# Modulation steps at six places of each feed-forward group, bias rows written in four pieces, and five operations moved to VectorE

## The chip, the cores and the metric

The kernel runs on one core of a Trainium2 chip. The core has five engines with an instruction queue each: TensorE (PE, matrix products; its weight loads are listed as PEld), VectorE (DVE), ScalarE (ACT), GpSimd (POOL) and SyncE (SP, which here only issues DMAs). Each engine takes its own instructions strictly in order; engines wait for one another through semaphores. The metric is the device time of one execution in microseconds (us).

## The reference

A diffusion backbone of two layers over 256 latent and 256 context tokens, width 1024, all in float32.

```python
def _swiglu(h, wg, wu, wd):
    return (jax.nn.silu(h @ wg) * (h @ wu)) @ wd

def reference(x, c, ctx, c_ctx, ...):
    for i in range(DEPTH):
        sh1, sc1, gt1, sh2, sc2, gt2 = _adaln(c, w_mod[i], b_mod[i])   # silu(c) @ w_mod + b_mod, six pieces
        cmod = _adaln(c_ctx, w_mod[i], b_mod[i])
        h_lat = _modulate(_rmsnorm(x, g_norm1[i]), sh1, sc1)
        h_ctx = _modulate(_rmsnorm(ctx, g_norm1[i]), cmod[0], cmod[1])
        if i % 2 == 0:
            y_lat, y_ctx = _mixer_ab(h_lat, h_ctx, ...)      # GQA beside chunked gated linear attention
            ffn = dense SwiGLU, D_FF = 3584
        else:
            y_lat, y_ctx = _mixer_c(h_lat, h_ctx, ...)       # neighbourhood attention + relative bias rpb_c
            ffn = top-2-of-8 expert SwiGLU
        x = x + gt1 * y_lat
        x = x + gt2 * ffn(_modulate(_rmsnorm(x, g_norm2[i]), sh2, sc2))
        ...                                                  # the same for ctx, in layer 0
    return _rmsnorm(x, g_final)
```

## The kernel before

The stages follow one another: layer 0's mixer (to about 345 us of the span), the dense feed-forward network (345 to 842), the norm of layer 1 and the projection of its values `vc` (842 to 910), neighbourhood attention (910 to 1060), router and experts (1060 to 1990).

A float32 product is written as three matmuls of rounded operands (`mm3`, L213 to L216; `mm3_features`, L476 to L481): high times high, high times low, low times high. So each weight tile is loaded (`raw`, a 1 MB DMA on SP's queue, L168), rounded on ACT (`whi`, L201), and its remainder is taken by one DVE subtraction of 2048 columns (`wlo`, L203). For four numbered tiles (`ON_POOL`: 8, 12, 57 and 71) the subtraction runs on POOL instead, in eight pieces of 256 columns (L209). Tile 8 is the first half of the weights of the `rb` projection (its matmuls write `pt_rb`); tile 57 is the second of the two weight tiles of the first half of `vc` (`pt_vc`).

The feed-forward network runs in seven groups (`NG`) of 512 hidden columns, about 62 us each. The up part of a group multiplies by gate and up weights (`pf_fg`, `pf_fu`), then `sg` (silu on ACT L965, product on DVE L966) and its two parts `fT` (L967, L968); the down part runs over four token blocks `t` and two halves: twelve matmuls into a bank `fd`, then `rtmp_ff` (DVE, L734, frees the bank) and `xr` (DVE, L735). A call of `tick()` in the group steps a generator: it computes three pieces of layer 1's modulation vector, pieces (1,0), (1,1) and (1,2). A piece takes ten steps: start the first 1 MB load of `w_mod`; eight chunks, in each of which DVE multiplies the chunk by a column of the condition and adds it into `acc` (L286 for the first, L288 after it; for piece (1,0) four half-wide operations, since both conditions need it); and an end with eight small matmuls into `mod_ps` (L294), `m_sb` (L301), four transposes `modT_ps` (L304) and two copies to `mT` (L308). Before, `tick()` stands behind each second `j` of an even group and behind each `j` of an odd one, twenty in all; `tick(24)` behind the loop runs what is left.

Then `norm_stream` makes layer 1's input for both token streams (transposes `tf_n` on PE, `f_hi` on ACT, `tfraw_n` on either, `f_lo` on DVE L380), and `proj_tokens` computes `vc` in two halves, each of two weight tiles. The relative bias goes a way of its own on POOL's queue: a table `rb_s` is zeroed (L997), sixteen small loads fill it (L999), one DMA writes each row 64 times to device memory as `rb_d` (L1000, 7168 rows of 512 bytes), each pair of heads reads its `bias` from there by four DMAs (L1055), and a window mask is added in three pieces on POOL (L1058). The zeroing and the load of the router's weights `wrA` are held until the write of `rb_d` is issued.

A scheduler orders the instructions of each engine; the code marked `ahead(PREP)` is weight preparation that it may issue early, and `issue_after(x)` holds an instruction until `x` has been issued.

## Time and profile before

| | us |
|---|---|
| three runs | 2011.80, 2011.66, 2010.35 |
| median | 2011.66 |
| the profiled execution | 2009.91 |
| its span in the trace | 2007.9 |
| PE busy | 1934.4 (96%) |
| DVE busy | 744.7 (37%) |
| ACT busy | 448.1 (22%) |
| POOL busy | 170.6 (8%) |

Times of the trace are us from the start of the span. A timeline row gives the start, the duration, engine, line, operation, `written<-read`, and in brackets the idle time of the engine just before it with what ended it. A matmul's duration is its whole way through the array; the step from one start to the next is what it costs in a row of matmuls. PE's granted clock is 1.00 at 2.4 GHz.

### The profile page before, as it was taken

The page shows a single profiled execution, that of the slowest core. Times are in us where ns is not written, and L with a number is a line of the kernel's source. Part 1 is how long each engine was busy: PE and PEld are TensorE (multiplying, and loading weights), DVE is VectorE, ACT ScalarE, POOL GpSimd, SP SyncE. Part 2 cuts the span into 40 slices and gives each one's busy share as a digit, 9 for nine tenths or more (in the row PEclk, how much of TensorE's full clock was granted, in tenths as well). Part 3 has the DMA queues.
Part 4 walks back from the last instruction along what each step waited for, and adds up shares of the span by engine and source line. Part 5 has one row for each costly group of instructions (what it writes and reads, how often), then busy time and mean ns, then how long its engine had stood idle before and what let it go on. Part 6 is the DMA issues. An engine that isn't in the chain of part 4 may idle for free.

```text
span 2007.9 us, 37143 instructions
## 1 busy us (share of the span) xinstructions
PE 1934.4 (96%) x16627; PEld 1180.6 (59%) x16627; DVE 744.7 (37%) x1185; ACT 448.1 (22%) x732; POOL 170.6 (8%) x203
## 2 busy tenths in 40 slices
PE   6998998999999999789999999999999999999996
PEld 3665676888878888567765354545444444544433
DVE  3246587576445643836773101111020101111022
ACT  4232265422222222235553010000100001010001
POOL 1103010000000000433311000000000100001010
PEclk9999999999999999899999999999999999999998
DMA  8624120454243442653338999999999999999991
GB/s 331 223 95 168 52 76 24 166 168 142 89 140 118 135 154 84 210 140 100 108 113 312 399 406 375 379 404 390 383 381 399 398 384 362 380 408 389 402 395 46
DMA packets 118901, 493.32 MB, mean 246 GB/s; under 512 B 10656, under 2 KB 50912, under 8 KB 98256
## 3 DMA queue, kind: packets, MB, share of 16 engines
q1 hardware_dynamic: 114096, 481.04, 63.2%
q0 software_dynamic: 3216, 7.03, 1.4%
q8 instruction: 132, 2.16, 0.4%
q10 hardware_dynamic: 1424, 2.81, 0.4%
q14 instruction: 33, 0.27, 0.0%
HBM read 486.13 MB, written 4.72 MB: 244 GB/s over the span
## 4 chain that ended last, share of the span: by engine, by line
PE 91%; DVE 3%; ACT 2%; issue 2%; DMA 1%; POOL 1%; ACTq 0%; SPq 0%; POOLq 0%; DVEq 0%
PE pu_e L1306 15%; PE pg_e L1306 14%; PE py_e L1306 14%; PE pf_fu L479 3%; PE pf_fu L480 3%; PE pf_fu L481 3%; PE pf_fg L479 3%; PE pf_fg L480 3%; PE pf_fg L481 3%; PE fd L216 2%; PE fd L215 2%; PE fd L214 2%; PE sc_e L1381 1%; PE mod_ps L253 1%; PE o_c L859 1%
## 5 line engine op out<-in xcount | busy, mean ns | idle before, releaser
L1306 PE MATMUL pu_e<-raw,X_all 128*32 128x448 f32 x3072 | 306.1, 540 | 0.0
L1306 PE MATMUL py_e<-raw,eT_e 128*32 128x256 f32 x5376 | 296.5, 379 | 0.0
L1306 PE MATMUL pg_e<-raw,X_all 128*32 128x448 f32 x3024 | 291.4, 539 | 0.0
L1306 PEld LDWEIGHTS py_e<-raw,eT_e 128*32 128x32 f32 x5376 | 190.4, 110 | 105.1 <-issue 5.1
L1306 PEld LDWEIGHTS pg_e<-raw,X_all 128*32 128x32 f32 x3024 | 100.0, 110 | 181.2 <-issue 175.6
L1306 PEld LDWEIGHTS pu_e<-raw,X_all 128*32 128x32 f32 x3072 | 98.4, 110 | 182.4 <-issue 178.6
L203 DVE TENSOR_TENSOR wlo<-raw,whi 128x2048 fp32r<-128x2048 f32 (+1 forms) x67 | 153.0, 2293 | 123.4 <-ACT whi L201 123.3
L201 ACT CAST whi<-raw 128x2048 fp32r<-128x2048 f32 (+1 forms) x73 | 135.0, 1859 | 262.4 <-PE fd L216 116.8
L1343 DVE TENSOR_TENSOR m_sb<-m_sb,pu_e 128x448 f32<-128x448 f32 x48 | 27.9, 604 | 393.5 <-PE pu_e L1306 393.4
L1339 ACT ACTIVATE m_sb<-pg_e 128x448 f32<-128x448 f32 x48 | 26.1, 543 | 512.8 <-PE pg_e L1306 512.8
L1384 POOL TENSOR_TENSOR xr<-xr,ytmp_e 128x512 f32<-128x512 f32 x28 | 35.2, 1277 | 822.5 <-DVE ytmp_e L1383 822.5
L481 PE MATMUL pf_fg<-f_hi,wlo 128*128 128x512 f32 (+1 forms) x240 | 92.2, 384 | 1.9 <-DVE wlo L203 1.9
L479 PE MATMUL pf_fg<-f_hi,whi 128*128 128x512 f32 (+1 forms) x240 | 93.1, 388 | 0.6 <-ACT whi L201 0.6
L214 PE MATMUL fd<-whi,fT 128*128 128x512 f32 x224 | 89.2, 398 | 4.3 <-DVE rtmp_ff L734 4.3
L480 PE MATMUL pf_fg<-f_lo,whi 128*128 128x512 f32 (+1 forms) x240 | 92.2, 384 | 0.2 <-DVE f_lo L380 0.2
L481 PE MATMUL pf_fu<-f_hi,wlo 128*128 128x512 f32 (+1 forms) x240 | 91.9, 383 | 0.0
L479 PE MATMUL pf_fu<-f_hi,whi 128*128 128x512 f32 (+1 forms) x240 | 91.2, 380 | 0.5 <-ACT whi L201 0.5
L480 PE MATMUL pf_fu<-f_lo,whi 128*128 128x512 f32 (+1 forms) x240 | 91.5, 381 | 0.0
L216 PE MATMUL fd<-whi,fT 128*128 128x512 f32 x224 | 89.6, 401 | 0.0
L215 PE MATMUL fd<-wlo,fT 128*128 128x512 f32 x224 | 89.3, 399 | 0.0
L1383 DVE SCALAR_TENSOR_TENSOR ytmp_e<-sc_e,comb,gate 128x512 f32<-128x512 f32 x32 | 23.6, 749 | 165.3 <-PE sc_e L1381 160.5
L1374 ACT COPY yF<-py_e 32x256 f32<-32x256 f32 x48 | 17.4, 362 | 265.9 <-PE py_e L1306 231.3
(375 smaller groups left out, 2715.9 us busy)
## 6 DMA issues: line engine op xcount, KB each, us to landing
raw<-in_w_moe_up_dram SPq DMA_DIRECT2D x128, 896.0 KB, 6.6
raw<-in_w_moe_down_dram SPq DMA_DIRECT2D x112, 1024.0 KB, 8.6
raw<-in_w_moe_gate_dram SPq DMA_DIRECT2D x126, 896.0 KB, 7.6
raw<-in_w_mod_dram SPq DMA_DIRECT2D x48, 1024.0 KB, 5.0
raw<-in_w_ff_gate_dram SPq DMA_DIRECT2D x14, 1024.0 KB, 5.0
raw<-in_w_ff_up_dram SPq DMA_DIRECT2D x14, 1024.0 KB, 5.0
raw<-in_w_ff_down_dram SPq DMA_DIRECT2D x14, 1024.0 KB, 4.8
raw<-in_w_in_c_dram SPq DMA_DIRECT2D x12, 1024.0 KB, 5.1
```

Source lines behind the costliest of these rows:

```text
L201: nc.scalar.copy(hi[:, c], raw[:, c])
L203: low.tensor_tensor(lo[:, c], raw[:, c], hi[:, c].bitcast(F32), op=ALU.subtract)
L214: nc.tensor.matmul(ps, ah, bh, start=start, stop=False)
L215: nc.tensor.matmul(ps, ah, bl, start=False, stop=False)
L216: nc.tensor.matmul(ps, al, bh, start=False, stop=stop)
L479: nc.tensor.matmul(ps, wh[:, k, ws], hh[:, k, ts], start=(k == 0), stop=False)
L480: nc.tensor.matmul(ps, wh[:, k, ws], hl[:, k, ts], start=False, stop=False)
L481: nc.tensor.matmul(ps, wl[:, k, ws], hh[:, k, ts], start=False, stop=(k == KT - 1))
L1306: nc.tensor.matmul(out[32 * q:32 * q + 32], lhsT, rhs[:, q], start=start, stop=stop, skip_group_check=True)
L1339: nc.scalar.activation(g, ps[s][:, 0:QW], AF.Silu)
L1343: nc.vector.tensor_tensor(gs[s], gs[s], ps[s][:, 0:QW], op=ALU.mult)
L1384: (nc.vector if self.last else nc.gpsimd).tensor_tensor(xr[2 + t][:, hs], xr[2 + t][:, hs], tmp, op=ALU.add)
```

## The change

1. `ON_POOL` keeps tiles 12 and 71. The subtractions of tiles 8 and 57 become one DVE instruction each.
2. `tick()` is called behind every `j` of the up part (four per group) and behind `t` = 1 and `t` = 3 of the down part, six per group; thirty steps are through within the fifth group.
3. `rb_s` is made before the feed-forward loop, and `rb_d` is written in four DMAs of 1792 rows on ACT's queue, in the sixth group, each behind a silu. `wrA` is no longer held.
4. The masks of the first three pairs are one DVE addition of 768 columns each, held until the last `f_lo`; the other five pairs stay on POOL.

```diff
@@ -154,6 +154,7 @@
     hi_tags = [(wpool, "whi", 2)]
     lo_tags = [(wpool, "wlo", 2)]
     state = {"n": 0, "r": 0, "c": 0}
+    critical = {}
 
     def pick(tags, n):
         seq = [t for t in tags for _ in range(t[2])]
@@ -170,7 +171,7 @@
 
     PREP = 500
 
-    ON_POOL = (8, 12, 57, 71)
+    ON_POOL = (12, 71)
 
     def load_split(src, shape, late=(), spare=False, raw=None, parts=None, pieces=1):
         with ahead(PREP):
@@ -377,7 +378,8 @@
                     nc.scalar.activation(rt, pv, AF.Identity, bias=B[:, f:f + 1], scale=A[:, f:f + 1])
                 else:
                     nc.vector.tensor_scalar(rt, pv, A[:, f:f + 1], B[:, f:f + 1], op0=ALU.mult, op1=ALU.add)
-                nc.vector.tensor_tensor(lo[:, f, :], rt, hi[:, f, :].bitcast(F32), op=ALU.subtract)
+                critical["normed"] = nc.vector.tensor_tensor(lo[:, f, :], rt, hi[:, f, :].bitcast(F32),
+                                                             op=ALU.subtract).ins
 
     streams = ((0, 1), (1, 0))
 
@@ -808,7 +810,6 @@
             nc.scalar.copy(qTt[:, 4 * g:4 * g + 4, :], ps.bitcast(F32).rearrange("p (h n) -> p h n", n=P))
         qT[t] = qTt
 
-    critical = {}
 
     class Heads:
 
@@ -946,6 +947,13 @@
     work["pool"] = fmp
     gates = [gate_rows(fmp, 0, 1, 5, "gate", 2), gate_rows(fmp, 0, 0, 5, "gate", 2)]
     ALL = slice(0, TOK)
+
+
+    rb_d = dram.tile([16 * 7, 64, P], F32, name="rb_d")
+    rb_s = fmp.tile([16 * 7, P], F32, name="rb_s")
+    nc.gpsimd.memset(rb_s, 0.0)
+    for h in range(16):
+        nc.gpsimd.dma_start(rb_s[7 * h:7 * h + 7, 48:79], rpb_c[0, h, 4:11, :])
     for g in range(NG):
         fT = [fmp.tile([P, 4, TOK], F32R, tag=f"fT{i}", bufs=2, name=f"fT{i}_{g}") for i in range(2)]
         for q in range(2):
@@ -962,12 +970,17 @@
                 j = 2 * q + m
                 pg, pu = pss[m]
                 sg = fmp.tile([P, 512], F32, tag="sg", bufs=2, name=f"sg{g}_{j}")
-                nc.scalar.activation(sg, pg, AF.Silu)
+                silu = nc.scalar.activation(sg, pg, AF.Silu).ins
                 nc.vector.tensor_tensor(sg, sg, pu, op=ALU.mult)
                 nc.scalar.copy(fT[0][:, j, :], sg)
                 nc.vector.tensor_tensor(fT[1][:, j, :], sg, fT[0][:, j, :].bitcast(F32), op=ALU.subtract)
-                if j % 2 or g % 2:
-                    tick()
+                tick()
+            if g == NG - 2:
+
+                for i in (2 * q, 2 * q + 1):
+                    with tc.issue_after(silu):
+                        nc.scalar.dma_start(rb_d[28 * i:28 * i + 28],
+                                            rb_s[28 * i:28 * i + 28].unsqueeze(1).to_broadcast([28, 64, P]))
         wd = [load_split(wdv[:, 4 * g + 2 * q:4 * g + 2 * q + 2, :], [P, 2, D]) for q in range(2)]
         for t in range(NT):
             for half in range(2):
@@ -978,6 +991,8 @@
                     sl = slice(t * P, (t + 1) * P)
                     mm3(ps, fT[0][:, j, sl], fT[1][:, j, sl], wh[:, j % 2, hs], wl[:, j % 2, hs], j == 0, j == 3)
                 add_residual(fmp, t, hs, ps, gates[t // 2], f"ff{g}_{t}_{half}")
+            if t % 2:
+                tick()
     tick(24)
     A3 = [scale_vec(1, cond, 1, 0, f"A3_{cond}") for cond in range(2)]
     for s, cond in streams:
@@ -988,17 +1003,7 @@
     mods.close()
 
 
-
-
-    rb_d = dram.tile([16 * 7, 64, P], F32, name="rb_d")
     psum_phase(p=2, s=3, t=2, o=1)
-    rbs = ExitStack()
-    rb_s = new_pool(rbs, "rbp", side="right").tile([16 * 7, P], F32, name="rb_s")
-    nc.gpsimd.memset(rb_s, 0.0)
-    for h in range(16):
-        nc.gpsimd.dma_start(rb_s[7 * h:7 * h + 7, 48:79], rpb_c[0, h, 4:11, :])
-    rb_ins = nc.gpsimd.dma_start(rb_d, rb_s.unsqueeze(1).to_broadcast([16 * 7, 64, P])).ins
-    rbs.close()
 
     na = ExitStack()
     n_hi, n_lo = f_hi, f_lo
@@ -1027,9 +1032,8 @@
     B4 = mod_vec(1, 0, 3)
     wrA = const.tile([P, KT, 32], F32, name="wrA")
     lgB = const.tile([P, NE], F32, name="lgB")
-    with tc.issue_after(rb_ins):
-        nc.gpsimd.memset(wrA, 0.0)
-        nc.gpsimd.dma_start(wrA[:, :, 0:NE], w_router[0].rearrange("(k p) e -> p k e", p=P))
+    nc.gpsimd.memset(wrA, 0.0)
+    nc.gpsimd.dma_start(wrA[:, :, 0:NE], w_router[0].rearrange("(k p) e -> p k e", p=P))
     lb_ps = bankB("lb_ps", "s")
     for k in range(KT):
         nc.tensor.matmul(lb_ps[:, 0:NE], B4[:, k:k + 1].to_broadcast([P, P]), wrA[:, k, 0:NE],
@@ -1054,9 +1058,14 @@
                                   [[P - 1, 64], [64 * P, 6], [1, 64]])
                     nc.gpsimd.dma_start(bias[64 * rr:64 * rr + 64, b], src)
         bv = bias.rearrange("p h m c -> p (h m) c")
-        for o in range(0, 12, 4):
-            nc.gpsimd.tensor_tensor(bv[:, o:o + 4], bv[:, o:o + 4],
-                                    cc(C_WIN, 64).unsqueeze(1).to_broadcast([P, 4, 64]), op=ALU.add)
+        if pair < 3:
+
+            with tc.issue_after(critical["normed"]):
+                nc.vector.tensor_tensor(bv, bv, cc(C_WIN, 64).unsqueeze(1).to_broadcast([P, 12, 64]), op=ALU.add)
+        else:
+            for o in range(0, 12, 4):
+                nc.gpsimd.tensor_tensor(bv[:, o:o + 4], bv[:, o:o + 4],
+                                        cc(C_WIN, 64).unsqueeze(1).to_broadcast([P, 4, 64]), op=ALU.add)
         pq = proj_features(wqk[pp][0], u2 * P, n_hi, n_lo, 256, f"cq{pair}", off=256)
         pk = proj_features(wqk[pp][1], u2 * P, n_hi, n_lo, TOK, f"ck{pair}")
         qk = []
```

Below, the order of the instructions on an engine, before and after. Names end in a number that tells tiles of one name apart.

VectorE in layer 0's projections, beside the first `rb` matmuls. `room` is the normalised and rotated query of a token block; `wlo_1128` is tile 9 (`wlo_1121` after), the second half of the `rb` weights. Before:

```order
L684 TENSOR_TENSOR room_87<-room_87,gqk 128x128
L692 TENSOR_TENSOR room_87<-room_87,cst_115 128x320 x2
L694 TENSOR_TENSOR room_87<-room_87,cst_115 128x640
L695 TENSOR_TENSOR room_87<-room_87 128x640
L203 TENSOR_TENSOR wlo_1128<-raw_1125,whi_1127 128x2048
L680 TENSOR_REDUCE ssq_3_1573<-room_87 128x10
```

After:

```order
L686 TENSOR_TENSOR room_87<-room_87,gqk 128x128
L694 TENSOR_TENSOR room_87<-room_87,cst_115 128x320 x2
L696 TENSOR_TENSOR room_87<-room_87,cst_115 128x640
L204 TENSOR_TENSOR wlo_1115<-raw_1112,whi_1114 128x2048
L697 TENSOR_TENSOR room_87<-room_87 128x640
L204 TENSOR_TENSOR wlo_1121<-raw_1118,whi_1120 128x2048
```

The first half's `wlo` (tile 8, `wlo_1115`) now stands on VectorE, one operation ahead of the end of the rotation.

VectorE at the end of the feed-forward network, in the down part of the last group. Before:

```order
L734 TENSOR_TENSOR rtmp_ff_0_0_5538<-fd_0_0_5525,gate_1_5_2744 128x512
L288 SCALAR_TENSOR_TENSOR acc_2_5653<-raw_5659,cT,acc_2_5653 128x2048
L735 TENSOR_TENSOR xr_1599<-xr_1599,rtmp_ff_0_0_5538 128x512
L288 SCALAR_TENSOR_TENSOR acc_2_5653<-raw_5662,cT,acc_2_5653 128x2048
L734 TENSOR_TENSOR rtmp_ff_0_1_5554<-fd_0_1_5541,gate_1_5_2744 128x512
L288 SCALAR_TENSOR_TENSOR acc_2_5653<-raw_5665,cT,acc_2_5653 128x2048
L735 TENSOR_TENSOR xr_1599<-xr_1599,rtmp_ff_0_1_5554 128x512
```

After, the last block of that part and the start of the norm (`wlo_5884` is tile 57):

```order
L736 TENSOR_TENSOR rtmp_ff_2_1_5672<-fd_2_1_5659,gate_0_5_2744 128x512
L737 TENSOR_TENSOR xr_1594<-xr_1594,rtmp_ff_2_1_5672 128x512
L347 TENSOR_SCALAR ms_n_1_0_5781<-ssq_n_1_0_5779 128x1
L736 TENSOR_TENSOR rtmp_ff_3_0_5688<-fd_3_0_5675,gate_0_5_2744 128x512
L361 TENSOR_SCALAR xc_5778<-xr_1594,rs_n_1_0_5783 128x1024
L737 TENSOR_TENSOR xr_1595<-xr_1595,rtmp_ff_3_0_5688 128x512
L736 TENSOR_TENSOR rtmp_ff_3_1_5704<-fd_3_1_5691,gate_0_5_2744 128x512
L204 TENSOR_TENSOR wlo_5884<-raw_5881,whi_5883 128x2048
L737 TENSOR_TENSOR xr_1595<-xr_1595,rtmp_ff_3_1_5704 128x512
L380 TENSOR_SCALAR tfraw_n_0_0_5732<-tf_n_0_0_5726,A_1_5709,mT_96 128x256
L381 TENSOR_TENSOR f_lo<-tfraw_n_0_0_5732,f_hi 128x256
```

No `acc` operation is left in this part; tile 57's `wlo` stands ahead of the last `xr`.

TensorE in the projection of `vc`, at the transposes of the second token stream (`tf_n_1_*`). Before:

```order
L216 MATMUL pt_vc_1_5903<-whi_5891,f_lo 128x512
L370 MATMUL tf_n_1_0_5777<-ident,xc_5762 128x128 x3
L370 MATMUL tf_n_1_1_5790<-ident,xc_5762 128x128 x3
L370 MATMUL tf_n_1_2_5803<-ident,xc_5762 128x128 x3
L370 MATMUL tf_n_1_3_5816<-ident,xc_5762 128x128 x4
L339 MATMUL gate_ps_0_2_0_6123<-m_sb_1595,ident 128x512
L339 MATMUL gate_ps_0_2_1_6126<-m_sb_1595,ident 128x512
L214 MATMUL pt_vc_2_5954<-whi_5885,f_hi 128x512
```

After:

```order
L371 MATMUL tf_n_1_0_5793<-ident,xc_5778 128x128 x4
L217 MATMUL pt_vc_0_5887<-whi_5877,f_lo 128x512
L217 MATMUL pt_vc_1_5888<-whi_5877,f_lo 128x512
L215 MATMUL pt_vc_1_5888<-whi_5877,f_hi 128x512
L371 MATMUL tf_n_1_1_5806<-ident,xc_5778 128x128 x4
L216 MATMUL pt_vc_1_5888<-wlo_5878,f_hi 128x512
L217 MATMUL pt_vc_1_5888<-whi_5877,f_lo 128x512
L215 MATMUL pt_vc_1_5888<-whi_5877,f_hi 128x512
L216 MATMUL pt_vc_1_5888<-wlo_5878,f_hi 128x512
L371 MATMUL tf_n_1_2_5819<-ident,xc_5778 128x128 x4
```

These transposes stood behind the first two blocks' matmuls in one run, and stand among them now.

## Rows read from the trace of the kernel before

**Rows 1.** Busy time by window: length, PE, PEld, DVE, ACT, POOL, clock, DMA share, GB/s

```profile
740.00:805.00 65.00, 65.00 (x281) 52.22 (x280) 28.05 (x30) 15.79 (x14) 0.00 (x0) 1.00 0.28 97
808.00:842.00 34.00, 28.86 (x122) 20.92 (x121) 31.47 (x32) 6.36 (x7) 8.82 (x17) 0.90 0.77 276
842.00:870.00 28.00, 19.85 (x87) 14.76 (x85) 17.90 (x34) 14.26 (x30) 12.49 (x17) 0.88 0.62 170
...
1075.00:1990.00 915.00, 912.80 (x11718) 412.98 (x11716) 109.08 (x211) 75.43 (x162) 40.26 (x32) 1.00 0.96 376
```

**Rows 2.** Timeline of PE, first `rb` matmuls

```profile
183.52 0.40 PE L214 MATMUL pt_rb<-whi,h_hi 128*128 128x512 f32 x1
...
192.28 0.80 PE L215 MATMUL pt_rb<-wlo,h_hi 128*128 128x512 f32 x1 [2.34 <-POOL wlo L209]
...
196.56 0.39 PE L216 MATMUL pt_rb<-whi,h_lo 128*128 128x512 f32 x1
```

**Rows 3.** Timeline of POOL and DVE, the same stretch

```profile
182.91 9.31 POOL L209 TENSOR_TENSOR wlo<-raw,whi 128x256 fp32r<-128x256 f32 x8 [1.48 <-ACT whi L201]
182.94 0.86 DVE L684 TENSOR_TENSOR room<-room,gqk 128x128 f32<-128x128 f32 x1
...
195.79 0.29 DVE L684 TENSOR_TENSOR room<-room,gqk 128x128 f32<-128x128 f32 x1
...
197.04 0.82 DVE L694 TENSOR_TENSOR room<-room,cst 128x640 f32<-128x640 f32 x1
```

**Rows 4.** Timeline of PE, down part of the last feed-forward group

```profile
808.01 0.40 PE L481 MATMUL pf_fu<-f_hi,wlo 128*128 128x512 f32 x1
...
826.49 0.50 PE L214 MATMUL fd<-whi,fT 128*128 128x512 f32 x1 [2.64 <-DVE rtmp_ff L734]
...
831.70 1.07 PE L294 MATMUL mod_ps<-acc,one_of 128*32 128x512 f32 x8 [0.85 <-DVE acc L288]
...
841.42 0.39 PE L216 MATMUL fd<-whi,fT 128*128 128x512 f32 x1
```

**Rows 5.** Costliest groups of DVE, 748 to 842: count, busy us, mean ns, idle

```profile
L288 DVE SCALAR_TENSOR_TENSOR acc<-raw,cT,acc 128x2048 f32<-128x2048 f32 x7 | 16.4, 2344 | 0.0
L203 DVE TENSOR_TENSOR wlo<-raw,whi 128x2048 fp32r<-128x2048 f32 x6 | 13.6, 2288 | 11.4 <-ACT whi L201 11.4
L734 DVE TENSOR_TENSOR rtmp_ff<-fd,gate 128x512 f32<-128x512 f32 x14 | 9.7, 689 | 7.2 <-PE fd L216 7.0
```

**Rows 6.** Timeline of PE, norm and `vc` projection

```profile
849.78 0.80 PE L216 MATMUL pt_vc<-whi,f_lo 128*128 128x512 f32 x1 [4.23 <-DVE f_lo L380]
...
866.32 0.66 PE L370 MATMUL tf_n<-ident,xc 128*128 128x128 f32 x4 [1.82 <-ACT tfraw_n L377]
...
870.61 0.50 PE L214 MATMUL pt_vc<-whi,f_hi 128*128 128x512 f32 x1 [1.92 <-ACT vc L1020]
...
884.26 0.50 PE L215 MATMUL pt_vc<-wlo,f_hi 128*128 128x512 f32 x1 [1.96 <-DVE wlo L203]
...
909.94 0.37 PE L479 MATMUL pf_cq<-f_hi,whi 128*128 128x256 f32 x1
```

**Rows 7.** Timeline of DVE and POOL, the same stretch

```profile
844.36 5.03 DVE L735 TENSOR_TENSOR xr<-xr,rtmp_ff 128x512 f32<-128x512 f32 x1
...
878.46 8.49 DVE L203 TENSOR_TENSOR wlo<-raw,whi 128x2048 fp32r<-128x2048 f32 x2 [7.91 <-ACT whi L201]
...
843.34 5.50 POOL L209 TENSOR_TENSOR wlo<-raw,whi 128x256 fp32r<-128x256 f32 x8
...
869.96 7.87 POOL L1055 DMA_DIRECT2D bias<-rb_d x12 [15.20 <-DMA rb_d<-rb_s]
877.84 10.39 POOL L1058 TENSOR_TENSOR bias<-bias,cst 128x256 f32<-128x256 f32 x9
```

**Rows 8.** POOL's issues of the `rb_s` loads, last feed-forward group

```profile
833.35 3.06 POOL L999 DMA_DIRECT2D rb_s<-in_rpb_c_dram  x6 [0.29 <-POOL rb_s L997]
```

**Rows 9.** DMA issues, 840 to 870: KB each, us from issue to landing

```profile
rb_d<-rb_s POOLq DMA_DIRECT2D x1, 3584.0 KB, 19.9
```

## The prediction

> **What bounds the kernel now.** The windows come first [rows 1]: inside the feed-forward loop PE has no idle time (65.00 of 65.00 us busy, 281 matmuls, so 0.231 us a step), and in the experts it is busy 912.80 of 915.00 us. There only fewer PE steps would help, and the change removes none. PE falls short in three short stretches, and the timelines of each show its waits. In the first `rb` matmuls PE waits piece after piece for POOL's `wlo` [rows 2, 3]. In the last down part VectorE is busy 31.47 of 34 us, PE waits for `rtmp_ff`, and the granted clock is 0.90 on average [rows 1, 4]. In the norm and the `vc` projection PE is idle 8.15 of 28 us at a granted clock of 0.88, with waits of 4.23, 1.82, 1.92 and 1.96 us [rows 1, 6]. The clock has two levels, 1.2 and 2.4 GHz; a mean of 0.90 over 34 us is about 6.8 us at the lower one. What the change is worth is read from these three stretches, plus what it puts into the loop and the stage before it.
>
> **Tile 8 on VectorE.** From 183.52 to 196.56 PE starts the first 21 `rb` matmuls, the last eleven from 192.28 on; with the last step that is 13.3 us, and 21 steps of 0.231 are 4.9, so 8.4 us are lost [rows 2]. POOL's eight pieces run 182.91 to 192.22 [rows 3]. In the new order VectorE reaches this `wlo` after L684, the two L692 and L694. Undisturbed, these take from 195.79 to 197.86, 2.07 us [rows 3]; beginning at 182.94 as now, `wlo` runs from 185.0 to 187.3 at 2.29 us each [rows 5]. PE can do one matmul, then waits from 183.75 to 187.3, 3.55 us. Behind the wait that ends at 192.28 the ten steps to 196.56 took 0.43 us each, the lower level [rows 2]; the same here adds 2.0 us. Lost after: 5.5 or, if the clock holds, about 3.9 (with 0.3 for the second half's `wlo`, which ends near 190.4). The gain is 2.9 or 4.5. I take 2.9: the matmul that ends a wait took 0.80 us behind 4.23 us and 0.50 behind the waits just under 2 [rows 6], and 3.55 is nearer to the former. The lower end is 1.0: L684 took 0.86 beside POOL's pieces against 0.29 without them [rows 3], and if VectorE were slow there for another reason, `wlo` would end 1.9 us later. The `rb` matmuls behind these wait for nothing else that moves, so the gain stays.
>
> The Trainium skill (SBUF — State Buffer, section "SBUF: two separate sides") says that VectorE operations with two inputs in SBUF and GpSimd operations exclude each other, the loser waiting for the whole instruction. Rows 3 agree (0.86 against 0.29), and so do rows 7, where `xr` took 5.03 us beside POOL's eight pieces. By this rule the upper value stands; without it the term would be 1.0.
>
> **Modulation steps earlier.** From the end of `pf_fu` (808.24) to the end of the last `fd` (841.65) are 33.4 us [rows 4] for 96 `fd` matmuls, 22.2 us at 0.231, and two ends of pieces. One `mod_ps` end takes 1.07 us [rows 4]; with half as much for its four transposes (an estimate by their count), two ends are 3.2. The other 8.0 us are waits for VectorE and the clock behind them. VectorE had seven L288 of 2.34 us in that stretch, between the `rtmp_ff` that free the banks [rows 5], and no idle time before them. After the change none of them is left in the last two groups. What remains there is eight `rtmp_ff` and eight `xr` of 0.69 us [rows 5], 11 us of the 22. So 8.0 us go; the 3.2 us of PE work only move into earlier groups, where PE is full, and cost there what they saved. SP's eight 1 MB loads leave the tail with them, so that `vc` weights are no longer queued behind them.
>
> **What this costs in the loop.** A group with six steps holds on VectorE six `wlo` (13.7 us), six L288 (14.1), eight operations on `sg` and `fT`, and sixteen `rtmp_ff` and `xr` (24 by 0.69, 16.6): 44 of some 62 us. It fits, but VectorE is in order. In the first group piece (1,0) costs two conditions a chunk, all eight chunks fall into that one group, and the wait of VectorE for a `w_mod` load holds the `wlo` and `sg` behind it. Going through the order with these durations, each `wlo` of group 0 still ends 0.2 to 2.8 us before PE needs it. No row prices the loss: below it is bounded by nothing, above by one L288 standing ahead of one `wlo`, 2.34 us. I take 1.0.
>
> **Tiles 57, bias rows and masks.** From 841.65 to the first `pf_cq` at 909.94 are 68.3 us [rows 6]. Up to 870 PE idles 8.15 us, and a clock of 0.88 costs 28 by 0.12, 3.4; after 870 come 0.6 (the rest of the wait that ends at 870.61) and 1.96: 14.1 in all, 54.2 of work at full speed. The 4.23 and 1.96 are POOL's: its `wlo` pieces stretched `xr` to 5.03, its masks stretched two `wlo` to 8.49 (4.58 undisturbed) [rows 7]. The 1.82 and 1.92 come from transposes that stand in one block with nothing between to hide the evictions; in the new order they stand among the `pt_vc` matmuls. What is late next: with T the end of the last `fd`, VectorE runs `rtmp_ff` to T+0.6, tile 57's `wlo` to T+2.9, `xr` to T+3.5, then `f_lo` (about 0.5, an estimate between 0.29 for 128 columns and 0.82 for 640 [rows 3]) to T+4.0. PE has work (eight transposes, a few matmuls) to about T+2.4, so it waits 1.6 to 2; smaller waits for later `f_lo` add 0.8. Total 2.8 where there were 14.1: gain 11.3. If the clock falls behind the first wait, ten steps cost 2.0 of it, 9.3. The waits of 1.82 to 1.96 us lie nearest, and two of them ended in matmuls of 0.50 us, not of 0.80 [rows 6], so I take 11.3.
>
> The masks, three operations of 768 columns at about 0.95 us (an estimate, L694's 0.82 by width), stand on VectorE between the later `wlo`, ahead of which it idled 7.91 us [rows 7]. They wait for `bias`, whose DMAs no longer wait 15.20 us for `rb_d` [rows 7]. `rb_d` itself took 19.9 us to landing [rows 9]; as four pieces on ACT in the sixth group, ACT issues four DMAs at 0.66 us (the price of POOL's `bias` issues, 7.87 for 12 [rows 7]), with nothing on ACT busy more than 15.79 of 65 us [rows 1]. Between nothing and, if ACT were held until each piece lands, 19.9/4 = 5.0 us apiece; the idle time of ACT covers either, so I take 0. The zeroing of `rb_s` and `wrA` on POOL meet an idle queue.
>
> **The sum.** 2.9 + 8.0 + 11.3 - 1.0 = 21.2. The profiled execution of 2009.91 (span 2007.9, 2.0 around it) would become 1988.7; it lay 1.75 below the median, so the median goes from 2011.66 to 1990.5. Ends of the terms: 1.0 + 8.0 + 9.3 - 2.3 = 16.0 and 4.5 + 8.0 + 11.3 = 23.8, so 1987.9 to 1995.7.
>
> **Rivals.** (a) The norm's hole is not closed but changes its owner. VectorE in order now carries tile 57's `wlo`, all `f_lo` and the masks; a mask that waits for a `bias` row would hold the `wlo` behind it, and PE would wait some 4.2 us as at 849.78 with 2.0 for the lower clock behind it, 6.2 us. For it: POOL's issue of twelve `bias` DMAs. Against: POOL issued six loads in 3.06 us, 0.5 each, while VectorE ran without a pause [rows 8]. One such loss leaves 15.0 of the gain, 1996.7; two leave 8.8, 2002.9.
>
> (b) VectorE falls behind in group 0 or in an odd place of the loop: a `wlo` late by two L288 is a wait of 4.7 us plus 2.0 for the clock, 6.7 instead of 1.0: 1996.2. For it: margins of 0.2 us. Against: 18 us of slack in each group.
>
> (c) Slower than before. The four pieces hold ACT or the weight loads in the sixth group. PE is at its limit there and every `whi` stands in ACT's queue behind a piece. A piece is 1792 rows of 512 bytes. If each kept ACT until landing, and landing beside weight loads took twice 5.0 us, four would be 40 us; buffers cover about one `whi` (1.9 us) and the idle time of ACT before it, some 5 us a piece, so 20 us of waiting plus 2.0 for the clock behind each, 28: 2018.5. It decides from 21.2 us on, 5.3 us a piece beyond its cover. Against: of the 19.9 us to the landing of the whole `rb_d`, POOL stood waiting for 15.20, and for the data alone [rows 7, 9]; it had gone on after the issue.
>
> The Trainium skill (DMA: Bandwidth & Descriptors, section "Queues, rings and completion order") says that each DMA engine takes turns between the queues by packet, so a load in flight would land later by up to the piece's own time. By that a piece costs a load at most 5 us, and no run here shows it.
>
> (d) The change doesn't reach the end: the experts are paced by DMA (share 0.96 [rows 1]) and an earlier start is eaten. Against: PE is busy 912.80 of 915 us there. It would give 2011.
>
> **How the numbers follow.** The forecast has 0.60, (a) 0.14, (b) 0.15, (c) 0.06, (d) 0.05. Of (a), three quarters lie at 1996.7 and the rest at 2002.9. What a measurement of this kernel can tell from no change is 0.2%, 4 us: faster is below 2007.6. So faster 0.89, same 0.05, slower 0.06. The range takes in the forecast's ends and (a) and (b) up to 2000: 1987 to 2000.
>
> **What would show it.** In the trace after: one PE wait of 3.5 us at the first `pt_rb` instead of four rising ones; the last down part 22 to 23 us long with VectorE half idle; from the last `fd` to `pf_cq` 56 to 60 us with no wait above 2.5; window 348 to 412 with PE idle no more than 1 us above before; ACT issuing four DMAs without a PE wait for `whi`. Wrong would be: waits for `wlo` in the first or sixth group, a `bias` mask heading VectorE's queue while `wlo` is due, or a gain of less than 15 us by the end of the norm.

## The result and the profile after

The changed kernel takes 1992.45 us (median of 1991.23, 1991.26, 1993.63, 1993.81), against 2011.08 for the kernel before: a ratio of 0.9905, interval 0.9893 to 0.9917. That is 18.6 us less; 1990.5 was predicted, in a range of 1987 to 2000. The profiled execution took 1991.23 us, its span is 1989.3.

First the ledger, from the starts of matmuls in the two traces. Each row is one stretch of PE's program. The last column is the prediction's term (a minus is a loss). The norm's row ends at `pf_ck` and not at `pf_cq`, because the changed kernel starts `pf_cq` ahead of some gate matmuls; up to `pf_ck` both do the same `vc`, gate and `pf_cq` matmuls.

| stretch | before, us | after, us | gain | predicted |
|---|---|---|---|---|
| span start to first `pt_rb` | 183.52 | 184.08 | -0.56 | 0 |
| first to last `pt_rb` | 56.23 | 54.03 | 2.20 | 2.9 |
| to first `pf_fg` | 104.65 | 104.34 | 0.31 | 0 |
| first `pf_fg` to first `fd` (first group) | 58.83 | 61.28 | -2.45 | -1.0 for the loop beyond 3.2 of moved matmuls |
| to last `pf_fu` (the other groups) | 404.78 | 408.58 | -3.80 | -3.2 |
| to last `fd` (last down part) | 33.41 | 22.28 | 11.13 | 8.0 + 3.2 |
| to first `pf_ck` (norm and `vc`) | 71.41 | 59.88 | 11.53 | 11.3 |
| to the first expert matmul | 165.53 | 165.49 | 0.04 | 0 |

Now the same places in the trace after. PE's timeline at the first `rb` matmuls: where POOL's pieces made four waits before, there is one of 3.35. Its end is a matmul of 0.80 us, and the steps behind it are 0.43 until 193.53: the lower clock (granted 0.50 in that stretch), as expected. The first three of the four waits before (the fourth is in [rows 2]):

```profile
184.45 0.50 PE L215 MATMUL pt_rb<-wlo,h_hi 128*128 128x512 f32 x1 [0.53 <-POOL wlo L209]
186.33 0.51 PE L215 MATMUL pt_rb<-wlo,h_hi 128*128 128x512 f32 x1 [0.91 <-POOL wlo L209]
188.86 0.50 PE L215 MATMUL pt_rb<-wlo,h_hi 128*128 128x512 f32 x1 [1.56 <-POOL wlo L209]
```

After:

```profile
184.08 0.40 PE L215 MATMUL pt_rb<-whi,h_hi 128*128 128x512 f32 x1
187.83 0.80 PE L216 MATMUL pt_rb<-wlo,h_hi 128*128 128x512 f32 x1 [3.35 <-DVE wlo L204]
188.42 0.63 PE L217 MATMUL pt_rb<-whi,h_lo 128*128 128x512 f32 x1
...
193.53 0.39 PE L217 MATMUL pt_rb<-whi,h_lo 128*128 128x512 f32 x1
```

VectorE there: without POOL's pieces L686 (L684 before) takes 0.28 us instead of the 0.86 of [rows 3], and `wlo` ends at 187.7.

```profile
183.50 0.28 DVE L686 TENSOR_TENSOR room<-room,gqk 128x128 f32<-128x128 f32 x1
...
185.49 2.28 DVE L204 TENSOR_TENSOR wlo<-raw,whi 128x2048 fp32r<-128x2048 f32 x1
```

Busy time by window after (columns as in [rows 1]). The first row is the first group, where PE is idle for 5.35 us (2.52 before, so more than the 1 us that the prediction allowed), the second the last down part, where PE is busy all 23 us at full clock and VectorE 15.5 instead of 31.5 of 34. The third is the norm, with 2.2 us of PE idle.

```profile
348.00:412.00 64.00, 58.65 (x326) 49.24 (x325) 57.03 (x50) 25.26 (x31) 8.02 (x16) 0.95 0.67 232
...
812.00:835.00 23.00, 23.00 (x102) 18.40 (x101) 15.52 (x23) 7.24 (x9) 1.66 (x3) 1.00 0.14 46
835.00:870.00 35.00, 32.79 (x155) 25.89 (x154) 21.46 (x34) 19.08 (x33) 8.39 (x13) 1.00 0.35 97
```

PE behind the last `fd` (834.59): the four waits of [rows 6] are one, 2.12 us.

```profile
834.59 0.39 PE L217 MATMUL fd<-whi,fT 128*128 128x512 f32 x1
...
839.48 0.73 PE L217 MATMUL pt_vc<-whi,f_lo 128*128 128x512 f32 x2 [2.12 <-DVE f_lo L381]
```

VectorE there. The last `xr` takes 0.69 us where it took 5.03 in [rows 7], the first `f_lo` stands behind tile 57's `wlo` as read from the order, and the first mask (0.95) ends 8 us before the `wlo` that follows it.

```profile
835.62 2.28 DVE L204 TENSOR_TENSOR wlo<-raw,whi 128x2048 fp32r<-128x2048 f32 x1
837.82 0.69 DVE L737 TENSOR_TENSOR xr<-xr,rtmp_ff 128x512 f32<-128x512 f32 x1
...
839.00 0.42 DVE L381 TENSOR_TENSOR f_lo<-tfraw_n,f_hi 128x256 fp32r<-128x256 f32 x1
...
851.30 0.95 DVE L1064 TENSOR_TENSOR bias<-bias,cst 128x768 f32<-128x768 f32 x1
860.40 2.29 DVE L204 TENSOR_TENSOR wlo<-raw,whi 128x2048 fp32r<-128x2048 f32 x1 [8.15 <-ACT whi L202]
```

The place that lost most beyond what was expected is the first group. PE's longest waits there after:

```profile
353.32 0.66 PE L371 MATMUL tf_n<-ident,xf 128*128 128x128 f32 x4 [1.87 <-ACT tfraw_n L378]
356.75 0.58 PE L481 MATMUL pf_fu<-f_hi,whi 128*128 128x256 f32 x1 [2.77 <-ACT whi L202]
```

The second of them was 0.48 us before:

```profile
358.66 0.38 PE L479 MATMUL pf_fu<-f_hi,whi 128*128 128x256 f32 x1 [0.48 <-ACT whi L201]
```

ScalarE's timeline says what that `whi` waited for after the change, a weight load:

```profile
354.80 1.90 ACT L202 CAST whi<-raw 128x2048 fp32r<-128x2048 f32 x1 [1.07 <-DMA raw<-in_w_ff_up_dram]
```

And SP's queue says why the load was late. After, two `w_mod` loads take the two free buffers, and gate and up weights start together at 345:

```profile
283.80 0.82 SPq L169 DMA_DIRECT2D raw<-in_w_mod_dram  x2
344.77 0.38 SPq L169 DMA_DIRECT2D raw<-in_w_ff_gate_dram  x1
345.24 0.53 SPq L169 DMA_DIRECT2D raw<-in_w_ff_up_dram  x1
```

Before, one `w_mod` load stood there, and the first gate weights were issued at 286, 59 us earlier:

```profile
285.45 0.34 SPq L168 DMA_DIRECT2D raw<-in_w_mod_dram  x1
285.89 0.39 SPq L168 DMA_DIRECT2D raw<-in_w_ff_gate_dram  x1
```

One more wait is new in the loop, at the start of the seventh group, behind the group with the four pieces of `rb_d`:

```profile
773.23 0.50 PE L481 MATMUL pf_fu<-f_hi,whi 128*128 128x512 f32 x1 [0.62 <-ACT whi L202]
```

It stands in every profiled run here that writes pieces on ScalarE's queue, and in none of the four that write `rb_d` another way (before, and the runs 'New tick places alone', 'Rows late' and 'Rows much earlier' below). In the two of these with six steps in every group and no other loss in the loop, the groups behind the first take 407.77 and 407.88 us instead of 408.58.

### The profile page after: what moved, and what is told of

It is laid out like the page before. It is cut to its first block, busy times and chain, and to the rows that moved or that the text cites. A ratio compares the mean times of both kernels' runs of the same rounds, so it can differ in the third digit from the quotient of the medians.

```text
span 1989.3 us, 37121 instructions
## 1 busy us (share of the span) xinstructions
PE 1926.8 (97%) x16627; PEld 1177.0 (59%) x16627; DVE 741.6 (37%) x1190; ACT 448.0 (23%) x732; POOL 142.7 (7%) x177
## 4 chain that ended last, share of the span: by engine, by line
PE 93%; DVE 2%; DMA 2%; ACT 1%; issue 1%; POOL 0%; SPq 0%; POOLq 0%; ACTq 0%; DVEq 0%
PE pu_e L1315 15%; PE pg_e L1315 15%; PE py_e L1315 15%; PE pf_fu L481 3%; PE pf_fu L482 3%; PE pf_fu L483 3%; PE pf_fg L481 3%; PE pf_fg L482 3%; PE pf_fg L483 3%; PE fd L217 3%; PE fd L215 2%; PE fd L216 2%; PE sc_e L1390 1%; PE mod_ps L254 1%; PE o_c L860 1%
```

## The experiments

Theory: the four gains and losses are those of the ledger, each with its own cause (tile 8's order on VectorE; the steps in the tail; tile 57 and the masks on POOL and late rows; the second `w_mod` load in the first group). The rivals of the prediction are tested beside it: (a) a mask holds VectorE's queue, (b) VectorE falls behind in the loop, (c) the pieces of `rb_d` hold ScalarE. Times are medians; where a stretch is given it is from the trace of that run, between the same matmuls as in the ledger, and 'changed' means the changed kernel.

### Tile 8 back on POOL

```diff
-    ON_POOL = (12, 71)
+    ON_POOL = (8, 12, 71)
```

> The changed kernel with tile 8's low part back on GpSimd, all else as changed. Theory: only the first rb matmuls change. PE's start of pt_rb to its last one goes back from 54.0 to 56.2 us, with four waits up to 2.3 us instead of one of 3.35; the run becomes 2.2 us slower than the changed kernel, about 1994.6. Rival: the wait of 3.35 us with 13 half-speed steps costs as much as the four did, and the 2.2 us seen between the two traces are noise of the stage: then no change, 1992.4.

Measured: 1994.97 us (ratio 0.9913). The `rb` stretch is 56.25 us, to 0.02 what it was before, and VectorE's short operation is stretched again:

```profile
183.33 0.86 DVE L686 TENSOR_TENSOR room<-room,gqk 128x128 f32<-128x128 f32 x1
```

The term is this tile's. Its size is 2.2 to 3.2 us: with tile 8 in one operation on VectorE the stretch took 54.0 to 54.1 us in five profiled runs, the changed kernel's among them, and 53.0 in the four others (last section).

### Tick places back

```diff
-                tick()
+                if j % 2 or g % 2:
+                    tick()
...
-            if t % 2:
-                tick()
```

> The changed kernel with tick() at the old places (behind each second j of even groups and each j of odd ones, none in the down part, the rest drained behind the loop). Theory: the last down part returns from 22.3 to about 33.4 us, the loop before it gets shorter by 3.2 us of modulation matmuls and by the 3 us that the first group lost, so 11.1 - 3.2 - 3.0 = 4.9 slower than the changed kernel, about 1997.3, and from the last fd to the first pf_ck about 60 us as in the changed kernel. Rival: the modulation steps in the tail were also what made the norm's start late, and the stretch behind the last fd grows too, by 4 or more: 2001 or more.

Measured: 1994.94 us (0.9914). The stretch behind the last `fd` stays at 59.94 us, so the rival falls. The first group is back at 58.70. But the last down part is 28.69 us, not 33.4, and so the loss is half of what was expected: the scheduler placed three of the last piece's eight chunks and the end of the piece before it ahead of that part, where the kernel before has all eight chunks and both ends in it. PE waits there 1.19 and 1.66 us, with the lower clock behind the second.

```profile
825.09 0.50 PE L215 MATMUL fd<-whi,fT 128*128 128x512 f32 x1 [1.19 <-DVE rtmp_ff L736]
828.04 1.07 PE L295 MATMUL mod_ps<-acc,one_of 128*32 128x512 f32 x8
830.76 0.66 PE L305 MATMUL modT_ps<-ident,m_sb 128*128 128x128 f32 x4 [1.66 <-DVE m_sb L302]
```

### New tick places alone

The kernel before with part 2 of the change only.

> The kernel before with the new tick() places alone: tiles 8 and 57, rb_d and the masks as before. Theory: the tail goes from 33.4 to 22.3 us, the loop before it grows by 6.2 (3.2 of moved matmuls, 3 of the first group); from the last fd to the first pf_ck the waits that POOL's wlo and masks made return, the wait for f_lo of 4 us with its clock and two late wlo, so 66 to 68 us instead of 71.4 before and 59.9 changed. Run 2011 - 4.9 - 4.4 = 2001.7. Rival: the whole stretch behind the last fd stays as before, 71.4, since rb_d, tile 57 and the masks were its only causes: 2006.

Measured: 2002.35 us (0.9955; 1997.28 in the profiled run, the other three 2001.9 to 2002.8, which no profile here explains). Tail 22.28, first group 61.48: as in the changed kernel. Behind the last `fd` 63.46 us, below what both theories said. One reason is in POOL's timeline: `rb_s` lies in memory that the modulation's accumulators free, so with the steps done early the old code writes `rb_d` at 713 us by itself.

```profile
700.92 0.21 POOL L998 MEMSET rb_s<- 112x128 f32 x1 [352.13 <-PE mod_ps L294]
...
712.96 2.47 POOL L1001 DMA_DIRECT2D rb_d<-rb_s  x1 [2.37 <-DMA rb_s<-in_rpb_c_dram]
```

Another is PE's order: the second stream's transposes stand among the `pt_vc` matmuls with this part alone. How much each is worth is not shown. So in this profiled run 8 of the 11.5 us behind the last `fd` come with the tick places too. The three unprofiled runs are 5 us slower, near the 2001.7 of the theory, and may have lost them in this stretch.

### Tile 57 back on POOL

```diff
-    ON_POOL = (12, 71)
+    ON_POOL = (12, 57, 71)
```

> The changed kernel with tile 57's low part back on GpSimd, its masks and all else as changed. Theory: the eight pieces stretch the last xr and the first f_lo behind it as in the kernel before; PE's wait for f_lo grows from 2.1 to about 4.2 us, and the lower clock behind it costs 2 us: from the last fd to the first pf_ck about 64 us instead of 59.9, the run about 1996.5. Rival: with no DMA issues and no acc operations beside it, POOL's pieces run while VectorE has little to do, and PE has no wait for that wlo: then f_lo comes 2.3 us earlier, the wait of 2.1 us goes and the run is 2 us faster, 1990.4.

Measured: 1996.06 us (0.9922); the stretch is 64.09 us, 4.2 more than changed, as the theory had it (3.1 more than in runs whose clock fell in this stretch, last section). Its path is another, though. `xr` takes only 1.16 us; it is POOL's own queue that is late. The `rs_n` of the last token block stands behind the eight pieces, VectorE's `xc` waits for it, and PE waits 3.52 us. POOL:

```profile
835.14 6.20 POOL L210 TENSOR_TENSOR wlo<-raw,whi 128x256 fp32r<-128x256 f32 x8 [2.73 <-ACT whi L202]
841.30 0.54 POOL L349 TENSOR_TENSOR rs_n<-ms_n,mhalf 128x1 f32<-128x1 f32 x1
```

VectorE, which waits for it:

```profile
841.88 0.75 DVE L361 TENSOR_SCALAR xc<-xr,rs_n 128x1024 f32<-128x1024 f32 x1 [4.10 <-POOL rs_n L349]
```

### Masks back on POOL

```diff
-        if pair < 3:
+        if pair < 0:
```

> The changed kernel with all masks on GpSimd again. Theory: the rows are there early, so GpSimd adds the masks at 13 to 24 us behind the last fd, when VectorE is through with most f_lo and before the wlo of the second vc half at 25.8; they stretch a few f_lo, which PE doesn't wait for by then: no change, within 1 us of 1992.4. Rival: the nine additions of 1.15 us take 10.4 us and reach into that wlo, stretching it as before (two took 8.49 us): a PE wait of 2 us and 1994.5.

Measured: 1997.05 us (0.9926; the profiled run 1993.20, the other three 1997.05 to 1997.08). In the profiled run the stretch is 62.02, 2.1 longer. Some 1.1 of it is not the masks': PE's steps are at the lower clock from 841 to 844 (granted 0.68 in 841 to 846), ahead of the first mask, as in runs that leave the masks alone (last section). The rest, about 1 us, is theirs: POOL's nine additions meet the last `f_lo` (pairs of them take 1.3 to 1.9 us instead of 0.75), and PE waits 0.64 us for a copy of `vc`. So the theory's 'within 1 us' just about holds in this run. The later `wlo`, which the rival had stretched, stay at 2.29 us. Why three runs are 3.9 us above the profiled one is open, and with it what the masks cost there.

```profile
848.46 7.87 POOL L1067 TENSOR_TENSOR bias<-bias,cst 128x256 f32<-128x256 f32 x9
```

### Rows late

One DMA on POOL's queue behind the last `rs_n` of the norm, in place of the four pieces:

```diff
-                        nc.scalar.dma_start(rb_d[28 * i:28 * i + 28], ...)
...
+    with tc.issue_after(critical["pow"]):
+        nc.gpsimd.dma_start(rb_d, rb_s.unsqueeze(1).to_broadcast([16 * 7, 64, P]))
```

> The changed kernel, but rb_d is written by one DMA on GpSimd's queue behind the last rs_n of the norm, 5 to 6 us behind the last fd, as late as in the kernel before; the masks stay on VectorE, where the first stands ahead of the wlo of the second vc half. Theory (the prediction's rival (a) as a mechanism): rb_d lands 20 us later, the first bias about 31 us behind the last fd, VectorE is held by the mask until then, the wlo behind it ends at about 34 where PE wants it at 29: a PE wait of 4 to 5 us and 2 us at the lower clock behind it, from the last fd to the first pf_ck 65 to 67 us instead of 59.9. The run comes to about 1998 to 1999. Rival: rb_d alone takes less than 20 us there, since it shared the DMA engines before; then the mask is ready by 25 us and nothing changes, 1992.4.

Measured: 1993.74 us (0.9908), the stretch 62.61 us. VectorE's queue does stand still for 12.71 us behind a mask, as rival (a) has it.

```profile
865.34 0.96 DVE L1060 TENSOR_TENSOR bias<-bias,cst 128x768 f32<-128x768 f32 x1 [12.71 <-DMA bias<-rb_d]
866.22 2.28 DVE L204 TENSOR_TENSOR wlo<-raw,whi 128x2048 fp32r<-128x2048 f32 x1
```

But PE never waits for that `wlo`. Its `whi` is done only at 865.87, so the mask held it for 0.4 us at most. PE's one new wait is 1.54 us, for ScalarE's copy of `vc`:

```profile
860.22 0.59 ACT L1021 COPY vc<-pt_vc 128x512 f32<-128x512 f32 x1 [7.57 <-issue]
```

PE:

```profile
860.86 0.50 PE L215 MATMUL pt_vc<-whi,f_hi 128*128 128x512 f32 x1 [1.54 <-ACT vc L1021]
```

`rb_d` was issued at 840.86 and took 19.2 us to landing, to 860.06; that ScalarE's copy was held by it is read from the times alone. So the late write cost 2.7 us in place of 5 to 7, of which about 1 is the clock (last section), and not by rival (a)'s path: that a held mask makes PE wait is not shown.

### Rows much earlier

The same DMA, meant to be held until the first `f_lo`. The hold named an instruction of VectorE and the DMA stands on POOL's queue; it held nothing, and the kernel wrote `rb_d` in one piece at 360 us, in the first group. The expectation is about something else than what ran.

> The changed kernel, but rb_d is written by one DMA on GpSimd's queue, held until the first f_lo of the norm, as late as in the kernel before. The masks stay on VectorE. Theory: bias rows land 29 us or more after the last fd, the first mask heads VectorE's queue, and the wlo of the q weights behind it comes some 4 us after PE wants it; with 2 us at the lower clock behind the wait the stretch to pf_ck grows by 4 to 7 us: 1996.5 to 1999.5. Rival: the masks on VectorE are harmless wherever the rows come, because the scheduler puts the wlo first: no change, 1992.4.

Measured: 1997.31 us (0.9928), and the run shows the cost of the place. The first group takes 66.95 us, 5.7 more than changed; the write takes 26.4 us to landing beside the first group's loads, VectorE waits 7.22 us for a `w_mod` load with `wlo` behind it, and PE's longest wait is this:

```profile
PE pf_fu L484 <- DVE wlo L204: 4.3, 1, 4.3
```

The stretch behind the last `fd` is 59.84, as in the changed kernel: early is all the masks need.

### Rows written twice

Each piece is followed by a second write of the same rows to a table that nobody reads.

```diff
+                    with tc.issue_after(silu):
+                        nc.scalar.dma_start(rb_e[28 * i:28 * i + 28], ...)
```

> The changed kernel, but each of the four pieces on ScalarE's queue is written twice, the second time to a table that nobody reads: double the issue and the transfer beside the sixth group's loads. Theory: ScalarE is held only for the issues of 0.8 us, and the loads of the sixth group (8.3 us to landing in the changed kernel beside a piece, against 5.0 alone) come another 3 us later, which is still covered by the buffers: no change, 1992.4. Rival (the prediction's (c)): with the second piece the cover of about 5 us is used up and PE waits for a whi at one to four places, 3 us each with the clock: 1995 to 2004.

Measured: 2002.46 us (0.9947): 10 slower than changed. The pieces do hold ScalarE, as the rival had it, though PE's new waits are not for a `whi`. In the changed kernel, ScalarE's issues are

```profile
717.42 0.92 ACTq L982 DMA_DIRECT2D rb_d<-rb_s  x1
...
723.43 0.83 ACTq L982 DMA_DIRECT2D rb_d<-rb_s  x1
...
744.95 0.81 ACTq L982 DMA_DIRECT2D rb_d<-rb_s  x1
...
750.34 0.80 ACTq L982 DMA_DIRECT2D rb_d<-rb_s  x1
```

at least 5.4 us apart, and each costs 0.8 to 0.9. The run with doubled writes has eight issues. The scheduler spread them, and those that begin 4.9 us or more behind the end of another still cost 0.8 to 0.9. Four follow within 0.3 us of the end of the one ahead; these take 3.9 to 6.8 us each, and ScalarE's `sg` and `fT` stand behind them. Three of the four:

```profile
744.46 0.81 ACTq L983 DMA_DIRECT2D rb_d<-rb_s  x1
745.31 5.65 ACTq L986 DMA_DIRECT2D rb_e<-rb_s  x1
...
751.22 6.78 ACTq L983 DMA_DIRECT2D rb_d<-rb_s  x1
...
758.08 3.94 ACTq L986 DMA_DIRECT2D rb_e<-rb_s  x1
```

PE then waits 3.01 us for `sg` and 1.66 for a `wlo`, and the clock falls behind the last (the 0.62 for a `whi` is in the changed kernel too). From the first `fd` to the last `pf_fu` are 416.80 us instead of 408.58; these 8.2 us are the writes'. The rest lies in two stretches that differ by as much in runs without this edit (last section).

```profile
751.66 0.50 PE L481 MATMUL pf_fg<-f_hi,whi 128*128 128x512 f32 x1 [3.01 <-ACT sg L974]
```

### The first group: four steps fewer, and one step fewer

```diff
-                tick()
+                if j % 2 or g:
+                    tick()
...
-            if t % 2:
+            if t % 2 and g:
                 tick()
```

> The changed kernel, but the first group has its two old tick() places; all other groups six. Theory: the first group's loss comes from the second w_mod load, which stands in SP's queue ahead of the first gate weight, so that gate and up weights are loaded together at 345 us and the third whi waits for DMA. Without that load, first pf_fg to first fd goes back from 61.3 to about 58.8 us, and the run is 2.5 to 3 us faster than the changed kernel, about 1989.7. Rival: the loss is VectorE's work (eight chunks in one group); then the chunks only move to the second group, where the same wait appears, and the time stays at 1992.4.

Measured: 1991.70 us (0.9899). The first group is back at 58.61 us: its loss came with the four steps. But 1.4 us go in the groups behind (410.00 instead of 408.58), where PE now waits 1.15 us for a `wlo` in the sixth group, into which the end of the last piece has moved. With one step fewer,

```diff
-                tick()
+                if g or j:
+                    tick()
```

> The changed kernel without the first tick() of the first group (five steps there, six in the others). Theory: SP's queue then has one w_mod load ahead of the first gate weight instead of two, so PE's waits for tf_n and whi in the first group shrink: first pf_fg to first fd about 58.7 us instead of 61.3; one step fewer in the group moves less work into the second group than leaving four out did, so most of it stays: 1990.2. Rival: VectorE's load in the first two groups sets the time, a wlo comes late in the second group as it did with two steps in the first, and less than 1 us stays: 1991.5 or more.

Measured: 1991.17 us (0.9901). SP's queue has one `w_mod` load ahead of the first gate weight again (issued at 282.91). First group 58.48, the others 408.77: 2.6 us of gain stay in the loop, and the load was the cause. The whole run shows about half of that, and by the whole time neither run can be told from the changed kernel. The profiled run lost 1.2 us behind the last `fd` and 1.6 on the way to the experts, and gained 1.0 at `rb`, stretches that the edit does not touch.

### Tile 8 in two halves

```diff
-                    low.tensor_tensor(lo[:, c], raw[:, c], hi[:, c].bitcast(F32), op=ALU.subtract)
+                    m = shape[1] // 2
+                    for d in ((slice(0, m), slice(m, shape[1])) if state["c"] == 8 else (c,)):
+                        low.tensor_tensor(lo[:, d], raw[:, d], hi[:, d].bitcast(F32), op=ALU.subtract)
```

> The changed kernel with tile 8's low part as two VectorE operations of 1024 columns instead of one of 2048. Theory: the first half is ready 1.1 us earlier, PE's wait at the first rb matmul is 2.2 us instead of 3.35, and the second half is done before PE asks for it: the rb stretch takes 52.9 us instead of 54.0, or 51 if the clock holds behind the shorter wait. Run 1991.3, or 1989.5. Rival: PE waits for the second half instead and the clock falls as before: within 0.5 us of 54.0, 1992.4.

Measured: 1989.10 us (0.9886, interval 0.9869 to 0.9902; all four runs, 1987.5 to 1989.6, lie below all four of the changed kernel). The wait is 2.28 us, the matmul that ends it takes 0.50 and the next step is at full speed: `rb` in 51.23 us, 2.8 less than changed, the better of the two values expected. The wait alone is 1.07 us shorter; the rest is the clock, which held in this run but not in the next one below. PE at that place:

```profile
186.60 0.50 PE L218 MATMUL pt_rb<-wlo,h_hi 128*128 128x512 f32 x1 [2.28 <-DVE wlo L206]
186.94 0.39 PE L219 MATMUL pt_rb<-whi,h_lo 128*128 128x512 f32 x1
```

### Both

> The two last edits together. Theory: they lie 160 us apart and add: 2.2 + 1.1 = 3.3 us faster than the changed kernel, about 1989.1. Rival: the order of the first group shifts with what comes ahead of it, and one of the two gains is lost: 1990.2 or more.

Measured: 1988.27 us (0.9884, interval 0.9868 to 0.9901), 4.2 us below the changed one by the medians, but not to be told from the halves alone (1989.10). The sum of 3.3 us expected is reached. In the profiled run `rb` takes 51.92 and the first group 59.82, so 2.1 and 1.5 us are kept. At `rb` the wait is the same as with the halves alone, but here the clock falls at once:

```profile
187.61 0.60 PE L218 MATMUL pt_rb<-wlo,h_hi 128*128 128x512 f32 x1 [2.29 <-DVE wlo L206]
188.00 0.63 PE L219 MATMUL pt_rb<-whi,h_lo 128*128 128x512 f32 x1
```

## Why the prediction was right, point by point

**Tile 8.** Predicted one wait of 3.55 us and the lower clock, 2.9 us gained. The wait was 3.35, the clock fell for 13 steps instead of ten, the gain 2.2; in four later profiles, where the same wait slowed eight or nine steps, it is 3.2. The reason (VectorE's operations shorten when POOL is quiet) is shown by L686: 0.28 us, and 0.86 again with tile 8 back on POOL. The value of 4.5 us, 'if the clock holds', appeared in no run with this wait.

**Steps out of the tail.** 8.0 us and 3.2 moved were predicted, 11.13 measured between the same matmuls [rows 4]. That the 3.2 reappear in the loop is right too: the groups behind the first are 3.8 longer, 3.0 to 3.1 in the two runs without the new wait for `whi`.

**The cost in the loop.** This is the term that was mis-sized: 1.0 us taken, 2.34 as the upper end, 3.05 measured (6.25 less 3.2), of which 2.45 in the first group. The other 0.6 is the size of that new wait, and the prediction put the pieces on ScalarE at nothing. The step that failed is the bound. It was taken from an operation on VectorE, but VectorE was not late in the first group; SP's queue was, with the second `w_mod` load in a buffer that the gate weights had held. The prediction counted the loads that leave the tail and not those that arrive at the front. The run with one step fewer shows it: 2.6 us come back. The row that stood for the loop, 740 to 805 without idle time [rows 1], does not cover the first group, where PE was idle for 2.52 us from 348 to 412 before the change already.

**Norm and `vc`.** 11.3 us predicted, 11.53 measured; the wait for `f_lo`, 1.6 to 2 us predicted, was 2.12, and the clock held. That it held is luck: behind the same wait it fell in six other profiled runs, at some 1.1 us each, and held in three. The size was right and the division partly wrong. Tile 57 is worth 3.1 to 4.2 us, yet in that run by way of `rs_n` in POOL's queue. The masks are worth about 1 in the one profile of them. The early rows came with the tick places too, because of the memory of `rb_s`; the prediction had them as a gain of the four pieces.

**Pieces on ScalarE.** Nothing was predicted; the wait of 0.62 us comes with them, against the sign named ('without a PE wait for `whi`'). How a piece leads to it is not shown. An issue takes 0.8 to 0.9 us, but the reason given (idle time of ScalarE covers any hold) is not what kept the pieces cheap. What did is the distance between the pieces. Rival (c), at 6 in 100, needed only twice the writes to appear, at about a third of its price. Two weight loads beside a piece took 8.3 and 6.5 us to landing instead of 5.0, a delay under the 5 us that the prediction allowed. The rule of the Trainium skill (DMA: Bandwidth & Descriptors, "Queues, rings and completion order") that queues share the DMA engines in turns fits these two delays.

**The rest.** Between the two profiled executions 21.2 us were predicted and 18.7 gained, 2.5 too few: 2.05 from the loop, 0.7 from tile 8, 0.56 from the stage ahead of `rb`, where the runs here scatter by 1 us without a change of theirs, less some gains of 0.2 to 0.3 that were not predicted. The median misses by 1.95, since the changed kernel's profile lay only 1.2 below its median. Rival (a) did not occur: POOL issued the twelve `bias` loads in 7.84 us, 0.65 each, beside a busy VectorE.

## What to carry to other kernels

A step that is moved out of a stretch brings its loads to where it goes: go through the load queue at the new place buffer by buffer, not only through the engine that does the arithmetic. An operation that another engine waits for should be cut where the waiting one can start on a part: 1024 columns instead of 2048 took the wait from 3.35 to 2.28 us, for one line; in one of two profiled runs the clock then held as well. DMAs with many small rows on a computing engine's queue were cheap here only while they were issued some us apart.

## What the runs showed of the hardware that was not expected

A DMA of 1792 rows of 512 bytes cost ScalarE 0.8 to 1.1 us to issue where the issue ahead of it had ended 4.5 us earlier or more, and 3.9 to 6.8 us where it had ended 0.3 us earlier or less; no run has a gap between. During the issue of 6.78 us at 751.22 ScalarE began one operation, 0.3 us after its start, and the next at 758.04.

The same wait doesn't always end in the same clock. Behind the same 2.12 us, the changed kernel stayed at the full clock (839.48, two matmuls in 0.73 us, above). The run with four steps fewer in the first group fell to the lower level (granted 0.63 from 838.6 to 843.2), which makes its stretch 60.98 us instead of 59.88:

```profile
838.61 1.22 PE L217 MATMUL pt_vc<-whi,f_lo 128*128 128x512 f32 x2 [2.12 <-DVE f_lo L381]
839.63 0.63 PE L215 MATMUL pt_vc<-whi,f_hi 128*128 128x512 f32 x1
```

At the first `rb` matmuls, behind the same 3.35 us, the steps slowed at once in the changed kernel (54.03 us) and after three or four full steps in four other runs (53.0). Such differences of 1.1 us, and one of 1.5 on the way to the experts that turned up in three of the runs, are as large as some of the effects looked for here, so edits of 1 to 2 us were judged by their own stretch and not by the whole time.
